# One-hot gate rows made token by token, and expert numbers found pair by pair, in a one-core PEER block

## The chip, the cores and the metric

The kernel runs on one core of a Trainium2 chip. The metric is device time in microseconds, as the median of several runs; lower is better. The engines are called by their names here: TensorE (PE in the profile, PEld for its weight loads), VectorE (DVE), ScalarE (ACT), GpSimd (POOL) and SyncE (SP), which issues most of the DMAs.

## The reference, cut to what matters

One layer of a bidirectional encoder: 512 tokens of width 1024 go through a mixer (a gated recurrence and a long convolution), and then through PEER, a channel mixer that looks up single-neuron experts. The change lies in PEER. For each token and each of 8 heads it finds the best 16 of 128 sub-keys in each of two halves, adds them to 256 candidate pairs, keeps the best 16 pairs, and so has 128 experts a token out of 16384, each with a softmax gate:

```python
s1, i1 = lax.top_k(s[:, :, 0], PEER_TOPK)
s2, i2 = lax.top_k(s[:, :, 1], PEER_TOPK)
cand_s = s1[..., :, None] + s2[..., None, :]          # 16 x 16 pairs
cand_i = i1[..., :, None] * PEER_NKEYS + i2[..., None, :]
top_s, pos = lax.top_k(cand_s, PEER_TOPK)
experts = jnp.take_along_axis(cand_i, pos, axis=-1)
g = jax.nn.softmax(top_s, axis=-1)
act = jax.nn.gelu(jnp.einsum('td,thkd->thk', xb, u[experts])) * g
out = jnp.einsum('thk,thkd->td', act, v[experts])
```

## The kernel before, in words

Four blocks of 128 tokens go through the layer. Block 0 (`GTB`) fetches its experts' rows by indirect DMA. Blocks 1 to 3 (`DTB`, 384 tokens) go the dense way: the products with all 16384 experts are made row by row (128 rows of 128 experts, `act_row`), a dense matrix of gates that is zero but for the chosen experts is multiplied in, and the rows of `v` are summed by matmuls into three accumulators (`combine`). All large matmuls are made of three passes with operands split in a high and a low part (`mm3`, `split`); the low parts are VectorE's work, except those of `uT` in the last loop, which are GpSimd's.

`top16` finds the best 16 of a row and their places by five VectorE operations. Only 50 of the 256 pairs can be among the best 16 (`PAIRS`), and a choice of rank under 8 only among the first 20 of them (`NFIRST`).

`select(tb, part)` serves half of the heads (4) of one token block, so it is called eight times. It adds up scores (`cs`) and expert numbers (`ci`) of the 50 pairs, takes the best 16 (`ctop`, `cpos`), makes the softmax `gate`, and then reads the expert number at each place. Before the change it does so for two heads and eight choices at a time: `one` compares the pair identities `pio` with the places (L1188), `exp` multiplies by `ci` (L1190), and a reduction over the pairs gives `eid` (L1181); the reductions run up to `ahead` groups later. A piece of it ends at each `yield`; the number that is yielded is a planner's cost.

`gates_out(k, tb)` turns the 128 experts and gates of each token into the token's 128 x 128 gate matrix. The expert number is parted in a row number `i1` and a column number `i2` (L1207 to L1211), both and the gates are transposed so that tokens lie along the free dimension (`tr` in bf16 for the numbers, `tg` for the gates), and then four tokens at a time are made: `one` compares the iota with both numbers (L1228), ScalarE turns the first half into `rows` (L1230), and VectorE multiplies the second half by the gates into `own` (L1231). Four blocks (`LAG`) later TensorE multiplies `own` and `rows` for each token (L1238), ScalarE copies the result to `Gs` (L1243), and SyncE's queue writes it to DRAM (`Gd`).

The order is set by generators. `queries` makes the sub-key scores and runs the first-half selections of blocks 1 and 2 beside them. Then `weave(main(), fill, PER)` (L894) runs the second-half selection of block 1 and `gates_out` for the three blocks, with the remaining selections put in after every third block of four tokens (`mixed`, L892), and lets one `act_row` in for each 2.4 units of the costs that are yielded. The last loop, `weave(rows(), gathered(), 1.0)` (L1023), runs all `combine` and the remaining `act_row` with the work of block 0 in between: its top-16 and its two selections (L917), then the indirect gathers (L906), one `scalar_tensor_tensor` with a written-out sum for each of 128 gathered rows of `u` (L931) and one for each of `v` (L940). An engine's queue runs in its order.

Of the kernel before, what the change touches and what calls it, by code (L numbers as in the profile page):

```python
# [9 lines left out]
F32 = mybir.dt.float32  # L10
# [11 lines left out]
P = 128  # L22
# [6 lines left out]
TOPK = 16  # L29
# [780 lines left out]
def peer(C, ctx, mh, ml):  # L810
# [6 lines left out]
    eid = cp.tile([P, TB, P], F32, name="eid")  # L817
    v16 = cp.tile([P, TB, 16, TOPK], F32, name="v16")
    i16 = cp.tile([P, TB, 16, TOPK], U32, name="i16")
    pio = cp.tile([P, NPAIR, TOPK // 2], BF16, name="pio")  # L820
    with tc.tile_pool(name="pid", bufs=1) as ip:
        pid = ip.tile([P, NPAIR], F32, name="pid")
        nc.scalar.dma_start(pid, a["pair"].to_broadcast([P, NPAIR]))
        nc.vector.tensor_copy(pio, pid[:, :, None].to_broadcast([P, NPAIR, TOPK // 2]))
    iota = cp.tile([P, P, 4], BF16, name="iota")
    nc.gpsimd.iota(iota, pattern=[[1, P], [0, 4]], base=0, channel_multiplier=0, allow_small_or_imprecise_dtypes=True)  # L826
    gidx = cp.tile([P, P], I32, name="gidx")
    gdot = cp.tile([P, P], F32, name="gdot")
    gw = cp.tile([P, P], F32, name="gw")
    def chosen(pool, tb, part, ahead=2):  # L830
        return select(C, pool, tb, part, v16, i16, gate, eid, pio, ahead)

    projected(C, mh, ml, xh, xl, xg)
    rowctx = ExitStack()
# [50 lines left out]
    with tc.tile_pool(name="slw", bufs=2) as sw, tc.tile_pool(name="gb", bufs=1) as gb, \  # L885
            tc.tile_pool(name="go", bufs=3) as go, tc.tile_pool(name="ps_g", bufs=5, space=PSUM) as ps_g:
        def main():
            rest = [[chosen(sw, tb, part) for part in range(2) if part or k >= EARLY] for k, tb in enumerate(DTB)]
            yield from chain(*rest[0])
            for k, tb in enumerate(DTB):  # L890
                nxt = chain(*rest[k + 1]) if k + 1 < len(DTB) else iter(())
                yield from mixed(gates_out(C, gb, go, ps_g, k, tb, gate, eid, iota), nxt, MIX)  # L892

        weave(main(), fill, PER)  # L894

# [14 lines left out]
    def gathered():  # L910

        for part in range(2):
            for hp in range(part * HEADS, part * HEADS + HEADS):
                top16(C, sw, v16[:, GTB, hp], i16[:, GTB, hp], s0[:, hp])
                if hp % 2:
                    yield 3.2
            yield from chosen(sw, GTB, part, 1)  # L917
        sgctx.close()
        nc.vector.tensor_copy(gidx, eid[:, GTB])
        swctx.close()  # L920
        gp = rowctx.enter_context(tc.tile_pool(name="gp", bufs=GBUFS))
        asked = chain(((a["u"], j) for j in range(P)), ((a["v"], j) for j in range(P)))
        there = [gather(gp, *q) for q in islice(asked, GAHEAD)]

        def row():
            there.extend(gather(gp, *q) for q in islice(asked, 1))
            return there.pop(0)

        for j in range(P):
            t = row()  # L930
            nc.vector.scalar_tensor_tensor(t, t, 1.0, xg, op0=ALU.mult, op1=ALU.mult, accum_out=gdot[:, j : j + 1])  # L931
            yield 1.2
        nc.scalar.activation(gw, gdot, AF.Gelu_apprx_tanh)
        nc.vector.tensor_mul(gw, gw, gate[:, GTB])
        for j in range(P):
            t = row()
            if j == 0:
                nc.vector.tensor_scalar(gacc, t, gw[:, 0:1], None, op0=ALU.mult)
            else:
                nc.vector.scalar_tensor_tensor(gacc, t, gw[:, j : j + 1], gacc, op0=ALU.mult, op1=ALU.add)  # L940
            yield 1.2
# [192 lines left out]
           for x in range(a0, a0 + na) for y in range(b0, b0 + nb)]  # L1134


def select(C, w2, tb, part, v16, i16, gate, eid, pio, ahead=2):

    nc = C.nc
    H = HEADS // 2  # L1140
    hs = slice(part * 2 * H, part * 2 * H + 2 * H)
    ks = slice(part * H * TOPK, part * H * TOPK + H * TOPK)
    i16f = w2.tile([P, 2 * H, TOPK], F32, name="i16f")
    nc.vector.tensor_copy(i16f, i16[:, tb, hs])
    ctop = w2.tile([P, H, TOPK], F32, name="ctop")
    cpos = w2.tile([P, H, TOPK], U32, name="cpos")
    cs = w2.tile([P, H, NPAIR], F32, name="cs")
    ci = w2.tile([P, H, NPAIR], F32, name="ci")
    i1x = w2.tile([P, H, TOPK], F32, name="i1x")
    vv = v16[:, tb, hs].rearrange("p (h q) k -> p h q k", q=2)  # L1150
    ii = i16f.rearrange("p (h q) k -> p h q k", q=2)
    nc.vector.tensor_scalar(i1x, ii[:, :, 0], 128.0, None, op0=ALU.mult)
    for dst, x1, x2, groups in ((cs, vv[:, :, 0], vv[:, :, 1], pair_groups(0, TOPK)[0]), (ci, i1x, ii[:, :, 1], FIRST + OTHERS)):
        for a0, na, b0, nb, off in groups:
            nc.vector.tensor_tensor(  # L1155
                dst[:, :, off : off + na * nb].rearrange("p h (a b) -> p h a b", b=nb),
                x1[:, :, a0 : a0 + na, None].to_broadcast([P, H, na, nb]),
                x2[:, :, None, b0 : b0 + nb].to_broadcast([P, H, na, nb]), op=ALU.add)
    yield 2.0
    for hd in range(H):  # L1160
        top16(C, w2, ctop[:, hd], cpos[:, hd], cs[:, hd])
    yield 2.5

    ex = w2.tile([P, H, TOPK], F32, name="ex")
    sm = w2.tile([P, H], F32, name="sm")
    mx = w2.tile([P, H], F32, name="mx")
    nc.vector.tensor_reduce(mx, ctop, axis=AX.X, op=ALU.max)
    nc.vector.tensor_tensor(ex, ctop, mx[:, :, None].to_broadcast([P, H, TOPK]), op=ALU.subtract)
    nc.scalar.activation(ex, ex, AF.Exp)
    nc.vector.reduce_sum(sm, ex, axis=AX.X)  # L1170
    nc.vector.reciprocal(sm, sm)
    nc.vector.tensor_tensor(gate[:, tb, ks].rearrange("p (h k) -> p h k", k=TOPK), ex,
                            sm[:, :, None].to_broadcast([P, H, TOPK]), op=ALU.mult)
    cpf = w2.tile([P, H, TOPK], BF16, name="cpf")
    nc.vector.tensor_copy(cpf, cpos)
    yield 1.0
    found = []

    def reduce():
        out, ex = found.pop(0)  # L1180
        nc.vector.reduce_sum(out, ex, axis=AX.X)  # L1181

    H2, K2 = 2, TOPK // 2
    for hd in range(0, H, H2):
        for k0, n in ((0, NFIRST), (K2, NPAIR)):
            one = w2.tile([P, H2, NPAIR, K2], BF16, name="one", bufs=2)
            ex = w2.tile([P, H2, K2, NPAIR], F32, name="exp", bufs=ahead + 1)
            nc.vector.tensor_tensor(one[:, :, :n], pio[:, None, :n].to_broadcast([P, H2, n, K2]),  # L1188
                                    cpf[:, hd : hd + H2, None, k0 : k0 + K2].to_broadcast([P, H2, n, K2]), op=ALU.is_equal)
            nc.vector.tensor_mul(ex[:, :, :, :n], one[:, :, :n].rearrange("p h j k -> p h k j"),  # L1190
                                 ci[:, hd : hd + H2, None, :n].to_broadcast([P, H2, K2, n]))
            out = eid[:, tb, ks].rearrange("p (h k) -> p h k", k=TOPK)[:, hd : hd + H2, k0 : k0 + K2]
            found.append((out, ex[:, :, :, :n]))
            if len(found) > ahead:
                reduce()
            yield 0.7 if k0 == 0 else 1.3
    while found:
        reduce()


def gates_out(C, gb, go, ps_g, k, tb, gate, eid, iota):

    nc = C.nc
    i1 = gb.tile([P, P], F32, name="i1")
# [5 lines left out]
    nc.vector.tensor_sub(i1, eid[:, tb], i2)  # L1210
    nc.vector.tensor_scalar(i1, i1, 1.0 / 128, None, op0=ALU.mult)  # L1211

    tr = gb.tile([P, P // 4, 2, 4], BF16, name="tr", bufs=2)
    tg = gb.tile([P, P], F32, name="tg", bufs=2)
    pt = ps_g.tile([P, 512], F32, name="ps_g")
    for j, src in enumerate((i1, i2, gate[:, tb])):
        nc.tensor.transpose(pt[:, j * P : j * P + P], src, C.ident)
    nc.scalar.copy(tr.rearrange("p b j t -> p j b t"), pt[:, : 2 * P].rearrange("p (j b t) -> p j b t", j=2, t=4))
    nc.scalar.copy(tg, pt[:, 2 * P : 3 * P])
    NB = P // 4  # L1220
    made, prods = {}, {}
    for b in range(NB + LAG + 1):
        if b < NB:

            one = go.tile([P, 2, P, 4], BF16, name="one", bufs=3)
            rows = go.tile([P, 4, P], F32, name="rows", bufs=LAG + 2)
            own = go.tile([P, 4, P], F32, name="own", bufs=LAG + 2)
            nc.vector.tensor_tensor(one, iota[:, None].to_broadcast([P, 2, P, 4]),  # L1228
                                    tr[:, b, :, None, :].to_broadcast([P, 2, P, 4]), op=ALU.is_equal)
            nc.scalar.copy(rows, one[:, 0].rearrange("p i t -> p t i"))  # L1230
            nc.vector.tensor_tensor(own, one[:, 1].rearrange("p i t -> p t i"),  # L1231
                                    tg[:, b * 4 : b * 4 + 4, None].to_broadcast([P, 4, P]), op=ALU.mult)
            made[b] = rows, own
        if LAG <= b < NB + LAG:
            rows, own = made.pop(b - LAG)
# [133 lines left out]
```

## Time and profile before

| | |
|---|---|
| time, median of 3 runs | 2113.68 us (2111.99 to 2114.71) |
| the profiled execution's own time | 2113.9 us |
| its span, first to last instruction | 2112.1 us |
| TensorE busy | 2058.7 us (97%) |
| VectorE busy | 1736.1 us (82%) |
| ScalarE busy | 978.6 us (46%) |
| GpSimd busy | 638.2 us (30%) |
| mean granted TensorE clock | 0.992 of full speed |

All stretches are in microseconds from the span's first instruction. A busy time is the union of the printed durations of an engine's instructions in a stretch; matmuls are pipelined, so that a busy TensorE is not TensorE at its peak. In a row of instructions "out<-in" are the kernel's names for the tiles, and "128x512 f32" is partitions by elements.

### The profile page before, as it was taken

The page shows a single profiled execution, that of the slowest core. Times are in us where ns is not written, and L with a number is a line of the kernel's source. Part 1 is how long each engine was busy: PE and PEld are TensorE (multiplying, and loading weights), DVE is VectorE, ACT ScalarE, POOL GpSimd, SP SyncE. Part 2 cuts the span into 40 slices and gives each one's busy share as a digit, 9 for nine tenths or more (in the row PEclk, how much of TensorE's full clock was granted, in tenths as well). Part 3 has the DMA queues.
Part 4 walks back from the last instruction along what each step waited for, and adds up shares of the span by engine and source line. Part 5 has one row for each costly group of instructions (what it writes and reads, how often), then busy time and mean ns, then how long its engine had stood idle before and what let it go on. Part 6 is the DMA issues. An engine that isn't in the chain of part 4 may idle for free. (4 is left out here: it accounts for less than half of the span.)

```text
span 2112.1 us, 29790 instructions
## 1 busy us (share of the span) xinstructions
PE 2058.7 (97%) x11109; PEld 1822.7 (86%) x11109; DVE 1736.1 (82%) x3073; ACT 978.6 (46%) x1396; POOL 638.2 (30%) x361
## 2 busy tenths in 40 slices
PE   7999999999999999979999999999999999999998
PEld 6888888888888898879988989989989998998997
DVE  6888764998998546999999988878878879778785
ACT  6555434667665623337766423333333333333333
POOL 0000000000000000000000378877777676666760
PEclk9999999999999999999999999999999999999999
DMA  6212222222212444124547689988888988888884
GB/s 199 80 51 66 70 70 94 67 65 66 70 54 81 120 151 139 61 70 168 202 180 250 192 311 344 327 318 304 321 318 301 317 311 299 316 317 324 296 286 148
DMA packets 153949, 407.68 MB, mean 193 GB/s; under 512 B 12457, under 2 KB 65451, under 8 KB 152140
## 3 DMA queue, kind: packets, MB, share of 16 engines
q1 hardware_dynamic: 110028, 255.98, 35.8%
q0 software_dynamic: 36864, 134.23, 17.6%
q10 hardware_dynamic: 6912, 15.56, 2.1%
q8 instruction: 87, 1.43, 0.3%
q14 instruction: 58, 0.48, 0.1%
HBM read 373.22 MB, written 32.51 MB: 192 GB/s over the span
## 5 line engine op out<-in xcount | busy, mean ns | idle before, releaser
L86 POOL TENSOR_TENSOR ul<-uraw,uh 128x1024 fp32r<-128x1024 f32 x100 | 265.3, 2654 | 589.7 <-DMA uraw<-in_uT 387.6
L95 PE MATMUL ps_a<-pxl,uh 128*128 128x384 f32 x1008 | 343.1, 340 | 0.0
L94 PE MATMUL ps_a<-pxh,uh 128*128 128x384 f32 x1008 | 341.8, 339 | 1.3 <-ACT gact L867 1.2
L980 PE MATMUL acc<-vl,gh 128*128 128x512 f32 x768 | 301.5, 393 | 2.1 <-DVE vl L86 2.1
L979 PE MATMUL acc<-vh,gh 128*128 128x512 f32 x768 | 299.7, 390 | 2.6 <-ACT vh L85 2.6
L981 PE MATMUL acc<-vh,gl 128*128 128x512 f32 x768 | 301.5, 393 | 0.0
L94 PE MATMUL ps_mm<-xh,whi 128*128 128x512 f32 (+1 forms) x656 | 259.1, 396 | 1.5 <-ACT xh L195 1.2
L940 DVE SCALAR_TENSOR_TENSOR xg<-grow,gw,xg 128x1024 f32<-128x1024 f32 x127 | 208.6, 1643 | 63.1 <-DMA grow<-in_v,gidx 62.0
L931 DVE SCALAR_TENSOR_TENSOR grow<-grow,xg 128x1024 f32<-128x1024 f32 x128 | 195.9, 1541 | 73.6 <-DMA grow<-in_u,gidx 73.3
L95 PE MATMUL ps_mm<-xl,whi 128*128 128x512 f32 (+1 forms) x656 | 255.0, 390 | 0.3 <-DVE xl L196 0.3
L85 ACT CAST vh<-vraw 128x1024 fp32r<-128x1024 f32 x128 | 134.3, 1050 | 252.7 <-PE acc L981 179.7
L826 POOL IOTA iota<- 128x512 bf16 x1 | 1.2, 1237 | 754.4 <-DVE gt L281 754.4
L906 POOL DMA_INDIRECT grow<-in_u,gidx x128 | 201.0, 1570 | 41.4 <-issue 19.4
L97 PE MATMUL ps_a<-pxh,ul 128*128 128x384 f32 x1008 | 200.1, 338 | 6.3 <-DVE ul L86 4.1
L85 ACT CAST uh<-uraw 128x1024 fp32r<-128x1024 f32 x128 | 134.7, 1053 | 143.5 <-PE ps_a L95 76.5
L94 PEld LDWEIGHTS ps_a<-pxh,uh 128*128 128x128 f32 x1008 | 191.1, 190 | 6.4 <-ACT gact L867 2.2
L95 PEld LDWEIGHTS ps_a<-pxl,uh 128*128 128x128 f32 x1008 | 190.9, 189 | 3.8
L86 DVE TENSOR_TENSOR vl<-vraw,vh 128x1024 fp32r<-128x1024 f32 x128 | 186.4, 1457 | 8.3 <-ACT vh L85 8.3
L97 PEld LDWEIGHTS ps_a<-pxh,ul 128*128 128x128 f32 x1008 | 176.8, 189 | 8.2 <-DVE ul L86 5.5
L906 POOL DMA_INDIRECT grow<-in_v,gidx x128 | 170.5, 1332 | 32.7 <-issue 18.3
L85 ACT CAST whi<-wraw 128x1024 fp32r<-128x1024 f32 x112 | 117.3, 1050 | 131.0 <-PE ps_mm L95 123.5
L980 PEld LDWEIGHTS acc<-vl,gh 128*128 128x128 f32 x768 | 144.6, 188 | 31.1 <-DVE vl L86 2.9
(414 smaller groups left out, 4188.8 us busy)
## 6 DMA issues: line engine op xcount, KB each, us to landing
uraw<-in_uT SPq DMA_DIRECT2D x128, 512.0 KB, 7.0
vraw<-in_v SPq DMA_DIRECT2D x128, 512.0 KB, 6.3
wraw<-in_w_in SPq DMA_DIRECT2D x80, 512.0 KB, 3.6
Gd<-Gs SPq DMA_DIRECT2D x12, 2048.0 KB, 7.2
gt<-Gd SPq DMA_DIRECT2D x32, 768.0 KB, 8.7
wraw<-in_w_q SPq DMA_DIRECT2D x16, 512.0 KB, 4.0
wraw<-in_w_b SPq DMA_DIRECT2D x8, 512.0 KB, 3.6
wraw<-in_w_a SPq DMA_DIRECT2D x8, 512.0 KB, 4.3
```

Of the source, the lines that this page charges most:

```text
L85: nc.scalar.copy(hi, src)
L86: return (eng or nc.vector).tensor_sub(lo, src, hi).ins
L94: nc.tensor.matmul(out, ah, bh, start=(i == 0), stop=False)
L95: nc.tensor.matmul(out, *((al, bh) if late else (ah, bl)), start=False, stop=False)
L97: nc.tensor.matmul(out, *((ah, bl) if late else (al, bh)), start=False, stop=(stop and i == n - 1))
L826: nc.gpsimd.iota(iota, pattern=[[1, P], [0, 4]], base=0, channel_multiplier=0, allow_small_or_imprecise_dtypes=True)
L906: nc.gpsimd.indirect_dma_start(out=t, out_offset=None, in_=tab, in_offset=bass.IndirectOffsetOnAxis(ap=gidx[:, j : j + 1], axis=0))
L931: nc.vector.scalar_tensor_tensor(t, t, 1.0, xg, op0=ALU.mult, op1=ALU.mult, accum_out=gdot[:, j : j + 1])
L940: nc.vector.scalar_tensor_tensor(gacc, t, gw[:, j : j + 1], gacc, op0=ALU.mult, op1=ALU.add)
L979: nc.tensor.matmul(acc[k][:, c], gh[:, ts_], vh[:, ds_], start=(r == 0), stop=False)
L980: nc.tensor.matmul(acc[k][:, c], gh[:, ts_], vl[:, ds_], start=False, stop=False)
L981: nc.tensor.matmul(acc[k][:, c], gl[:, ts_], vh[:, ds_], start=False, stop=(r == NK - 1))
```

## The change

In `gates_out` the one-hot for the column number is no longer compared four tokens at a time and then multiplied: one `tensor_scalar` per token compares a row of numbers 0 to 127 (`line`) with the token's column number and multiplies by its gate, both read from memory as one value per partition. `one` shrinks to the half that `rows` needs. In `select` the three steps over groups become one `scalar_tensor_tensor` for each head and choice: compare the pair identities with the place, multiply by the expert numbers, and write out the sum.

```diff
@@ -817,18 +817,17 @@
     eid = cp.tile([P, TB, P], F32, name="eid")
     v16 = cp.tile([P, TB, 16, TOPK], F32, name="v16")
     i16 = cp.tile([P, TB, 16, TOPK], U32, name="i16")
-    pio = cp.tile([P, NPAIR, TOPK // 2], BF16, name="pio")
-    with tc.tile_pool(name="pid", bufs=1) as ip:
-        pid = ip.tile([P, NPAIR], F32, name="pid")
-        nc.scalar.dma_start(pid, a["pair"].to_broadcast([P, NPAIR]))
-        nc.vector.tensor_copy(pio, pid[:, :, None].to_broadcast([P, NPAIR, TOPK // 2]))
+    pio = cp.tile([P, NPAIR], F32, name="pio")
+    nc.scalar.dma_start(pio, a["pair"].to_broadcast([P, NPAIR]))
     iota = cp.tile([P, P, 4], BF16, name="iota")
     nc.gpsimd.iota(iota, pattern=[[1, P], [0, 4]], base=0, channel_multiplier=0, allow_small_or_imprecise_dtypes=True)
+    line = cp.tile([P, P], F32, name="line")
+    nc.gpsimd.iota(line, pattern=[[1, P]], base=0, channel_multiplier=0, allow_small_or_imprecise_dtypes=True)
     gidx = cp.tile([P, P], I32, name="gidx")
     gdot = cp.tile([P, P], F32, name="gdot")
     gw = cp.tile([P, P], F32, name="gw")
-    def chosen(pool, tb, part, ahead=2):
-        return select(C, pool, tb, part, v16, i16, gate, eid, pio, ahead)
+    def chosen(pool, tb, part):
+        return select(C, pool, tb, part, v16, i16, gate, eid, pio)
 
     projected(C, mh, ml, xh, xl, xg)
     rowctx = ExitStack()
@@ -889,7 +888,7 @@
             yield from chain(*rest[0])
             for k, tb in enumerate(DTB):
                 nxt = chain(*rest[k + 1]) if k + 1 < len(DTB) else iter(())
-                yield from mixed(gates_out(C, gb, go, ps_g, k, tb, gate, eid, iota), nxt, MIX)
+                yield from mixed(gates_out(C, gb, go, ps_g, k, tb, gate, eid, iota, line), nxt, MIX)
 
         weave(main(), fill, PER)
 
@@ -914,7 +913,7 @@
                 top16(C, sw, v16[:, GTB, hp], i16[:, GTB, hp], s0[:, hp])
                 if hp % 2:
                     yield 3.2
-            yield from chosen(sw, GTB, part, 1)
+            yield from chosen(sw, GTB, part)
         sgctx.close()
         nc.vector.tensor_copy(gidx, eid[:, GTB])
         swctx.close()
@@ -1134,7 +1133,7 @@
            for x in range(a0, a0 + na) for y in range(b0, b0 + nb)]
 
 
-def select(C, w2, tb, part, v16, i16, gate, eid, pio, ahead=2):
+def select(C, w2, tb, part, v16, i16, gate, eid, pio):
 
     nc = C.nc
     H = HEADS // 2
@@ -1171,34 +1170,21 @@
     nc.vector.reciprocal(sm, sm)
     nc.vector.tensor_tensor(gate[:, tb, ks].rearrange("p (h k) -> p h k", k=TOPK), ex,
                             sm[:, :, None].to_broadcast([P, H, TOPK]), op=ALU.mult)
-    cpf = w2.tile([P, H, TOPK], BF16, name="cpf")
+    cpf = w2.tile([P, H, TOPK], F32, name="cpf")
     nc.vector.tensor_copy(cpf, cpos)
     yield 1.0
-    found = []
-
-    def reduce():
-        out, ex = found.pop(0)
-        nc.vector.reduce_sum(out, ex, axis=AX.X)
-
-    H2, K2 = 2, TOPK // 2
-    for hd in range(0, H, H2):
-        for k0, n in ((0, NFIRST), (K2, NPAIR)):
-            one = w2.tile([P, H2, NPAIR, K2], BF16, name="one", bufs=2)
-            ex = w2.tile([P, H2, K2, NPAIR], F32, name="exp", bufs=ahead + 1)
-            nc.vector.tensor_tensor(one[:, :, :n], pio[:, None, :n].to_broadcast([P, H2, n, K2]),
-                                    cpf[:, hd : hd + H2, None, k0 : k0 + K2].to_broadcast([P, H2, n, K2]), op=ALU.is_equal)
-            nc.vector.tensor_mul(ex[:, :, :, :n], one[:, :, :n].rearrange("p h j k -> p h k j"),
-                                 ci[:, hd : hd + H2, None, :n].to_broadcast([P, H2, K2, n]))
-            out = eid[:, tb, ks].rearrange("p (h k) -> p h k", k=TOPK)[:, hd : hd + H2, k0 : k0 + K2]
-            found.append((out, ex[:, :, :, :n]))
-            if len(found) > ahead:
-                reduce()
-            yield 0.7 if k0 == 0 else 1.3
-    while found:
-        reduce()
-
-
-def gates_out(C, gb, go, ps_g, k, tb, gate, eid, iota):
+
+    out = eid[:, tb, ks].rearrange("p (h k) -> p h k", k=TOPK)
+    for hd in range(H):
+        for k in range(TOPK):
+            n = NFIRST if k < TOPK // 2 else NPAIR
+            own = w2.tile([P, NPAIR], F32, name="own", bufs=4)
+            nc.vector.scalar_tensor_tensor(own[:, :n], pio[:, :n], cpf[:, hd, k : k + 1], ci[:, hd, :n],
+                                           op0=ALU.is_equal, op1=ALU.mult, accum_out=out[:, hd, k : k + 1])
+        yield 0.9
+
+
+def gates_out(C, gb, go, ps_g, k, tb, gate, eid, iota, line):
 
     nc = C.nc
     i1 = gb.tile([P, P], F32, name="i1")
@@ -1210,26 +1196,26 @@
     nc.vector.tensor_sub(i1, eid[:, tb], i2)
     nc.vector.tensor_scalar(i1, i1, 1.0 / 128, None, op0=ALU.mult)
 
-    tr = gb.tile([P, P // 4, 2, 4], BF16, name="tr", bufs=2)
-    tg = gb.tile([P, P], F32, name="tg", bufs=2)
+    tr = gb.tile([P, P // 4, 4], BF16, name="tr", bufs=2)
+    tg = gb.tile([P, 2, P], F32, name="tg", bufs=2)
     pt = ps_g.tile([P, 512], F32, name="ps_g")
     for j, src in enumerate((i1, i2, gate[:, tb])):
         nc.tensor.transpose(pt[:, j * P : j * P + P], src, C.ident)
-    nc.scalar.copy(tr.rearrange("p b j t -> p j b t"), pt[:, : 2 * P].rearrange("p (j b t) -> p j b t", j=2, t=4))
-    nc.scalar.copy(tg, pt[:, 2 * P : 3 * P])
+    nc.scalar.copy(tr, pt[:, :P].rearrange("p (b t) -> p b t", t=4))
+    nc.scalar.copy(tg, pt[:, P : 3 * P].rearrange("p (j t) -> p j t", j=2))
     NB = P // 4
     made, prods = {}, {}
     for b in range(NB + LAG + 1):
         if b < NB:
 
-            one = go.tile([P, 2, P, 4], BF16, name="one", bufs=3)
+            one = go.tile([P, P, 4], BF16, name="one", bufs=3)
             rows = go.tile([P, 4, P], F32, name="rows", bufs=LAG + 2)
             own = go.tile([P, 4, P], F32, name="own", bufs=LAG + 2)
-            nc.vector.tensor_tensor(one, iota[:, None].to_broadcast([P, 2, P, 4]),
-                                    tr[:, b, :, None, :].to_broadcast([P, 2, P, 4]), op=ALU.is_equal)
-            nc.scalar.copy(rows, one[:, 0].rearrange("p i t -> p t i"))
-            nc.vector.tensor_tensor(own, one[:, 1].rearrange("p i t -> p t i"),
-                                    tg[:, b * 4 : b * 4 + 4, None].to_broadcast([P, 4, P]), op=ALU.mult)
+            nc.vector.tensor_tensor(one, iota, tr[:, b, None, :].to_broadcast([P, P, 4]), op=ALU.is_equal)
+            nc.scalar.copy(rows, one.rearrange("p i t -> p t i"))
+            for q in range(4):
+                t = b * 4 + q
+                nc.vector.tensor_scalar(own[:, q], line, tg[:, 0, t : t + 1], tg[:, 1, t : t + 1], op0=ALU.is_equal, op1=ALU.mult)
             made[b] = rows, own
         if LAG <= b < NB + LAG:
             rows, own = made.pop(b - LAG)
```

## Rows read from the trace of the kernel before

**Rows 1.** The busy line of the page: busy us (share of the span) xinstructions.
```profile
PE 2058.7 (97%) x11109; PEld 1822.7 (86%) x11109; DVE 1736.1 (82%) x3073; ACT 978.6 (46%) x1396; POOL 638.2 (30%) x361
```

**Rows 2.** Busy time by stage: us, PE, PEld, DVE, ACT, POOL, PEclk, DMA share, GB/s.
```profile
870.00:948.00 78.00, 68.87 (x352) 60.24 (x350) 78.00 (x368) 26.86 (x44) 0.00 (x0) 0.98 0.19 63
948.00:1136.00 188.00, 178.77 (x1237) 170.38 (x1238) 186.39 (x463) 144.19 (x245) 0.00 (x0) 0.96 0.51 189
1136.00:1160.00 24.00, 20.57 (x117) 19.93 (x115) 23.49 (x113) 9.29 (x12) 4.86 (x2) 0.99 0.85 296
1300.00:2000.00 700.00, 700.00 (x3496) 631.62 (x3496) 571.88 (x500) 250.31 (x294) 505.24 (x287) 1.00 0.88 315
```

**Rows 3.** The chain that ended last, in order of time: start us, us, what.
```profile
1133.71 0.53 DVE i L1254 x2
...
1159.66 1.12 DVE vl L86
1160.83 0.80 PE acc L980
...
1221.59 8.25 DMA grow<-in_u,gidx
```

**Rows 4.** VectorE in order of time, blocks of `gates_out`: start us, us printed, instruction.
```profile
953.18 1.29 DVE L1231 TENSOR_TENSOR own<-one,tg 128x512 f32<-128x512 bf16 x2
954.39 1.28 DVE L1228 TENSOR_TENSOR one<-iota,tr 128x1024 bf16<-128x1024 bf16 x2
955.59 1.28 DVE L1231 TENSOR_TENSOR own<-one,tg 128x512 f32<-128x512 bf16 x2
```

**Rows 5.** VectorE groups by form, whole span: count, busy us, mean ns, idle before.
```profile
L1231 DVE TENSOR_TENSOR own<-one,tg 128x512 f32<-128x512 bf16 x96 | 62.6, 682 | 0.0
L1228 DVE TENSOR_TENSOR one<-iota,tr 128x1024 bf16<-128x1024 bf16 x96 | 62.4, 682 | 0.4 <-ACT rows L1230 0.4
```

**Rows 6.** VectorE in order of time, ahead of the first gate block.
```profile
949.21 0.21 DVE L1211 TENSOR_SCALAR i<-i 128x128 f32<-128x128 f32 x1
949.34 1.04 DVE L1155 TENSOR_TENSOR ci<-i1x,i16f 128x32 f32<-128x32 f32 x11
```

**Rows 7.** VectorE groups by form, relatives of the new instructions, whole span.
```profile
L748 DVE SCALAR_TENSOR_TENSOR ya<-hrs,vec,so 128x512 f32<-128x512 f32 x8 | 5.9, 741 | 0.0
L747 DVE TENSOR_TENSOR hrs<-ps_x,hrs 128x512 f32<-128x512 f32 x8 | 5.5, 683 | 1.0 <-ACT hrs L116 1.0
...
L1155 DVE TENSOR_TENSOR ci<-i1x,i16f 128x8 f32<-128x8 f32 x16 | 1.9, 164 | 0.0
...
L375 DVE TENSOR_SCALAR arg<-ps_x,vec 64x512 f32<-64x512 f32 x2 | 1.6, 800 | 3.5 <-PE ps_x L389 3.5
```

**Rows 8.** VectorE groups by form in 870 to 948 us, the selection's.
```profile
L1190 DVE TENSOR_TENSOR exp<-one,ci 128x800 f32<-128x800 bf16 x6 | 9.6, 1596 | 0.0
...
L1181 DVE TENSOR_REDUCE eid<-exp 128x16 f32<-128x800 f32 x6 | 5.9, 978 | 0.0
L1190 DVE TENSOR_TENSOR exp<-one,ci 128x320 f32<-128x320 bf16 x6 | 4.3, 718 | 0.0
L1188 DVE TENSOR_TENSOR one<-pio,cpf 128x800 bf16<-128x800 bf16 x6 | 3.4, 568 | 0.0
L1181 DVE TENSOR_REDUCE eid<-exp 128x16 f32<-128x320 f32 x6 | 2.8, 471 | 0.0
...
L1188 DVE TENSOR_TENSOR one<-pio,cpf 128x320 bf16<-128x320 bf16 x6 | 1.9, 315 | 0.0
```

**Rows 9.** VectorE in order of time, an instruction with a sum in the last loop.
```profile
1238.00 1.21 DVE L86 TENSOR_TENSOR vl<-vraw,vh 128x1024 fp32r<-128x1024 f32 x1
1239.13 1.21 DVE L931 SCALAR_TENSOR_TENSOR grow<-grow,xg 128x1024 f32<-128x1024 f32 x1
1240.28 0.08 DVE L931 DVE_READ_ACCUMULATOR grow<-grow,xg 128x1 f32 x1
1240.28 1.22 DVE L931 SCALAR_TENSOR_TENSOR grow<-grow,xg 128x1024 f32<-128x1024 f32 x1
```

## The prediction

> **What bounds the kernel now.** I read the busy line of the page first. TensorE is busy 97% of the span, VectorE 82% [rows 1]. A mean over the span hides the stage that matters, so the second view was the busy time by stages, cut where the lines of the diff begin and end. From 870 to 948 us (two of the early selections and the third) VectorE is busy 78.00 of 78 us and TensorE 68.87. From 948 to 1136 us (the gate matrices) VectorE has 186.39 of 188 and TensorE 178.77. From 1136 to 1160 us it is 23.49 of 24 against 20.57, and in the steady part behind it TensorE has no gap while VectorE has room [rows 2]. So the reader sees one engine full for 290 us, and that is VectorE, with TensorE close behind. The third view was the chain of waits: from 1133.71 us it runs from one VectorE instruction to the next, until `vl` at 1159.66 releases the first product of the last loop; at 1221.59 it runs through the first gathered row, and that gather cannot start until the expert numbers of token block 0 are known [rows 3]. Everything the diff touches on VectorE lies between 870 and 1221 us. I take it that a microsecond added there is a microsecond at the end, while a microsecond removed is worth at most what TensorE idles.
>
> **The unit of the sum.** A printed duration is longer than the place that an instruction takes. Two `own` in a row are printed as 1.29 us, yet the next pair starts 1.21 us behind them [rows 4]. So neighbours overlap by 0.08 us, and I count start to start. Two `one` and two `own` take 955.59 - 953.18 = 2.41 us, 1.205 us for a block of four tokens [rows 4]; there are 96 of each [rows 5].
>
> **Gate matrices, `gates_out`.** Removed per block: one `one` over 1024 and one `own` over 512 elements, 1.205 us. Added: `one` over 512 elements, and four `tensor_scalar` over 128 elements with two scalars read from memory each. The 1024 bf16 elements take no longer than 512 f32 ones, two a cycle, and the new `one` has the same inner pattern; 256 cycles fewer at 0.96 a ns are 0.267 us off 0.60, which leaves 0.333. The plain 128-element f32 `tensor_scalar` with constants starts at 949.21 and its follower at 949.34: 0.13 us [rows 6]. What the scalars from memory add is read from longer relatives: 512 elements with one such scalar take 741 ns against 683 without (58 more), and the one `tensor_scalar` with two takes 800, 117 above the 683 of a one-a-cycle instruction [rows 7]. So an `own` of one token takes 0.13 + 0.12 = 0.25 us, four take 1.00, and the block 1.333 us: 0.128 more than before. Times 96: **+12.3 us**. Bounds: below, the scalars cost nothing in a short instruction (0.853 a block, -33.8 us); above, the comparison with two scalars runs at one element a cycle, 64 cycles or 0.067 us more four times (+25.6 on top, +37.9). I take the middle because the row with two scalars is the nearest, and it shows them paid in full.
>
> **Expert numbers, `select`.** Eight calls, two for each token block. Removed per call: two rounds of six instructions, printed 315, 718, 471, 568, 1596 and 978 ns [rows 8], 4.65 us, less six overlaps of 0.08, so 4.17 a round and 8.33 a call. Added per call: 64 `scalar_tensor_tensor` (4 heads by 16 choices), 32 over 20 pairs and 32 over 50, each with one scalar from memory and a sum written out. The smallest two-input instruction has 8 elements and takes 164 ns [rows 7], so 156 ns are there before the first element. With 1.04 ns an element and 58 for the scalar, less 80 of overlap, 20 pairs take 0.155 us and 50 take 0.186: 32 x 0.341 = 10.9 us. The sum is a second instruction, the accumulator read. Behind the 1024-element relative it is printed with 0.08 us, but the next instruction starts at the same moment, and start to start is 1.15 against 1.13 for the `vl` without a sum [rows 9], so I count 0.008 each, 0.5 us a call. That makes 11.4 a call, 3.1 more than before; eight calls, **+24.7 us**. Bounds: below, a free scalar (7.2 us, -1.1 a call, -9); above, the accumulator read takes its own 0.08 behind a short instruction, where no long stream covers it (+4.4 a call, +35 on top).
>
> The Vector Engine (DVE) Microarchitecture Reference of the Trainium skill ("Points that are easy to get wrong") says that a scalar-tensor-tensor with two SBUF sources that are not bf16 runs at half throughput, since no read port is left for the accumulator; the new instruction is of that kind. The row of 1024 elements has two such sources and a sum, and its 1.15 us are one element a cycle, so the trace disagrees. By that rule the eight calls would cost 8 x 2240 elements x 1.04 ns = 18.6 us more.
>
> **Edits that I cost at nothing.** The cast of `pio` (0.4 us) goes from VectorE, well ahead of the full stretch; I leave it out. The second iota is GpSimd's, which is idle until the last loop [rows 2]. The copies on ScalarE swap widths (`tr` half, `tg` double) and keep their count. Half of the `one` being gone, `rows` may start 0.27 us earlier; nothing comes of it, because VectorE fills that time. No wait is added: the products still run four blocks behind `own`. The weights that the selection yields fall from 4.0 to 3.6, which moves the total that paces the fill rows from 55.9 to 55.3; divided by 2.4, both give 23 rows. The same DMAs are issued in the same order.
>
> **Sum.** 12.3 + 24.7 = 37 us on VectorE. Three selections (9.3) fall into 870 to 948 us and three (9.3) with the gates (12.3) into 948 to 1136, both full. The last two (6.2) stand ahead of the first gather, and `vl` of the following rows is queued behind the instruction that waits for that gather. So nothing hides them: where TensorE now idles 9 us in each of the first two stages it will idle longer. The profiled execution took 2113.9 us (span 2112.1), 0.2 above the median of the three runs. 2113.9 + 37 = 2151; the removed cast and the few tenths in which VectorE does wait today make it **2150 us**.
>
> **Rivals.**
> A. The accumulation is dearer than the long row shows: the read takes its 0.08 us each time (2150 + 35 = 2185), or, as the page's rule would have it, the stream runs at half speed (2150 + 19 = 2169). For it: the read is an instruction of its own with a printed time, and a 20-element stream is shorter than that. Against it: behind 1024 elements it leaves no trace. An `own` at one element a cycle (+26, 2176) has the same sign and size.
> B. The second scalar is free: `own` takes 0.19 us, the block 1.093, and the gates gain 10.8 us instead of losing 12.3. Then 2150 - 23 = 2127. For it: two scalars could be fetched together. Against it: 117 ns is twice 58.
> C. Faster: the scalars of a short instruction are fetched under its predecessor, as its start-up partly is. Then the block takes 0.853 us and a call 7.2, and VectorE loses 43 us of work. The gain is cut off by TensorE: 9.2 us idle in 948 to 1136, 3.4 from three selections before, 2.3 from the two behind; 15 us, 2099. It decides where a 128-element `own` gets below 0.22 us and a pair instruction below 0.13. Against it: both rows with scalars show them paid although a full instruction ran ahead of them.
> D. VectorE's longer queue is hidden: TensorE, not VectorE, holds the stage from 948 to 1136, since the two are 8 us apart, and the selections are caught up later in the loop, where VectorE has 18% free. Then only what exceeds TensorE's gaps counts and about 2115 comes out. Against it: the chain at 1133 to 1160 is VectorE alone, and the first product waits for it.
>
> **How the numbers follow.** The forecast has 0.58 (2134 to 2163 its own range), A 0.18, B 0.11, C 0.07, D 0.06. The range 2122 to 2188 takes in A and B and leaves out C and D and a heap of A's prices. Within 0.2% is 2109.5 to 2117.9, about what a measurement of this kernel can tell from no change. Faster gets 0.07 (C), the same 0.06 (D), slower 0.87.
>
> **What would show it.** In the profile of the changed kernel: `own` of one token at 0.32 us printed and 0.25 start to start; pair instructions at 0.155 and 0.186 start to start, and the accumulator read printed without moving its follower; 870 to 948 longer by about 9 us, the gate stage by about 21, with TensorE's idle time there up by as much; the loop behind the first gather as long as now. If start to start of `own` is under 0.22, or the first `vl` stands no later than 1159.66, the argument is wrong.

## The result and the profile after

The changed kernel takes 2141.06 us (median of 4 runs, 2139.92 to 2141.78), the kernel before 2114.19 on the same chip: 1.0128 times as long, interval 1.0111 to 1.0146, or 27 us. The forecast was 2150, 37 us more. The profiled execution took 2141.01 us, span 2139.2.

The busy line, which answers to [rows 1]; VectorE has 20.6 us more, TensorE the same share:
```profile
PE 2065.9 (97%) x11109; PEld 1824.2 (85%) x11109; DVE 1756.7 (82%) x4288; ACT 982.4 (46%) x1396; POOL 634.3 (30%) x362
```
The busy time by stages (columns as in [rows 2]), cut where the same work begins and ends:
```profile
870.00:966.00 96.00, 85.11 (x413) 74.13 (x412) 93.25 (x774) 28.88 (x49) 0.00 (x0) 0.93 0.16 52
966.00:1177.00 211.00, 184.59 (x1226) 169.11 (x1226) 209.48 (x1099) 148.36 (x246) 0.00 (x0) 0.98 0.45 169
1177.00:1201.00 24.00, 21.07 (x122) 20.68 (x120) 23.89 (x156) 9.91 (x13) 7.21 (x3) 1.00 0.69 257
1300.00:2000.00 700.00, 699.82 (x3517) 633.46 (x3516) 572.51 (x520) 253.28 (x298) 510.83 (x290) 1.00 0.90 319
```
VectorE is still the full engine there, and TensorE's idle time in the gate stage has grown from 9.2 us [rows 2] to 26.4. Ahead of the gate stage it has hardly grown, from 9.1 to 10.9. The new instructions as groups by form (count, busy us, mean ns printed), the answer to [rows 5, 8]:
```profile
L1218 DVE TENSOR_SCALAR own<-line,tg 128x128 f32<-128x128 f32 x384 | 109.5, 366 | 0.0
L1182 DVE SCALAR_TENSOR_TENSOR own<-pio,cpf,ci 128x50 f32<-128x50 f32 x256 | 54.6, 289 | 0.0
L1182 DVE SCALAR_TENSOR_TENSOR own<-pio,cpf,ci 128x20 f32<-128x20 f32 x256 | 53.6, 279 | 0.0
L1182 DVE DVE_READ_ACCUMULATOR own<-pio,cpf,ci 128x1 f32 x512 | 49.0, 96 | 0.0
L1214 DVE TENSOR_TENSOR one<-iota,tr 128x512 bf16<-128x512 bf16 x96 | 42.4, 442 | 0.0
```
Read by printed means, one block would take 0.442 + 4 x 0.366 = 1.9 us. The order in time tells another price (start us, us printed):
```profile
1005.40 0.25 DVE L1182 SCALAR_TENSOR_TENSOR own<-pio,cpf,ci 128x20 f32<-128x20 f32 x1
1005.55 0.10 DVE L1182 DVE_READ_ACCUMULATOR own<-pio,cpf,ci 128x1 f32 x1
1005.55 0.25 DVE L1182 SCALAR_TENSOR_TENSOR own<-pio,cpf,ci 128x20 f32<-128x20 f32 x1
...
1006.87 0.29 DVE L1182 SCALAR_TENSOR_TENSOR own<-pio,cpf,ci 128x50 f32<-128x50 f32 x1
1007.06 0.10 DVE L1182 DVE_READ_ACCUMULATOR own<-pio,cpf,ci 128x1 f32 x1
1007.06 0.29 DVE L1182 SCALAR_TENSOR_TENSOR own<-pio,cpf,ci 128x50 f32<-128x50 f32 x1
...
1008.21 0.44 DVE L1214 TENSOR_TENSOR one<-iota,tr 128x512 bf16<-128x512 bf16 x1
1008.55 1.13 DVE L1218 TENSOR_SCALAR own<-line,tg 128x128 f32<-128x128 f32 x4
1009.57 0.44 DVE L1214 TENSOR_TENSOR one<-iota,tr 128x512 bf16<-128x512 bf16 x1
```
From one `one` to the next is 1009.57 - 1008.21 = 1.36 us (1.205 before [rows 4]); four `own` take 1.02 of it, 0.256 each. A pair instruction takes 0.160 us for 20 pairs and 0.192 for 50, and its accumulator read starts together with the next pair instruction: it takes no place at all. A call comes to 32 x 0.352 = 11.26 us.

Where the 27 us arise is read from four marks, in tile views (least, median and longest ns; first and last start). Before:
```profile
L1228 DVE TENSOR_TENSOR one<-iota,tr x96: 670/680/704, 952.0 to 1130.7; 128x1024 bf16<-128x1024 bf16 x96
L919 DVE CAST gidx<-eid x1: 213/213/213, 1221.1 to 1221.1; 128x128 int32<-128x128 f32 x1
L979 PE MATMUL acc<-vh,gh x768: 387/389/632, 1158.7 to 2103.8; 128*128 128x512 f32 x192
```
And after:
```profile
L1214 DVE TENSOR_TENSOR one<-iota,tr x96: 405/438/476, 968.2 to 1171.7; 128x512 bf16<-128x512 bf16 x96
L918 DVE CAST gidx<-eid x1: 223/223/223, 1254.5 to 1254.5; 128x128 int32<-128x128 f32 x1
L978 PE MATMUL acc<-vh,gh x768: 389/389/628, 1200.7 to 2130.9; 128*128 128x512 f32 x192
```
The first gate block is 16.2 us late, the last 41.0, the first product of the last loop 42.0, the gather's indices (`gidx`) 33.4, the last product 27.1. So VectorE's price arrives in full, and more, at the last loop; 9 us come back before the gather and 6 behind it.

Of the first 16.2 us, 6 are there before any of the changed VectorE instructions runs; 1.4 of these 6 stand already in the mixer, where the two kernels do the same work (its `yb` starts at 296.1 us against 294.7 before). ScalarE's queue in the kernel before (`ACTq` rows are DMA issues):
```profile
703.07 0.33 ACTq L823 DMA_DIRECT2D pid<-in_pair  x1
...
753.30 0.33 ACTq L1069 DMA_DIRECT2D h<-in_x  x1
```
The same queue after:
```profile
756.03 0.33 ACTq L821 DMA_DIRECT2D pio<-in_pair  x1
756.40 0.46 ACTq L1063 DMA_DIRECT2D gfn<-in_g_ffn  x1
756.47 0.61 ACT L85 CAST mgh<-gt 128x512 fp32r<-128x512 f32 x1
756.88 1.04 ACTq L1068 DMA_DIRECT2D h<-in_x  x2
```
And what waits for `h` (idle time before an instruction, and its releaser, in brackets): VectorE before, VectorE after, then TensorE after:
```profile
758.64 0.88 DVE L1074 TENSOR_TENSOR h<-ps_mm,h 128x256 f32<-128x256 f32 x2
```
```profile
765.92 1.09 DVE L1073 TENSOR_TENSOR h<-ps_mm,h 128x256 f32<-128x256 f32 x3 [7.06 <-DMA h<-in_x]
```
```profile
766.40 0.58 PE L94 MATMUL ps_mm<-woh,mgh 128*128 128x256 f32 x1 [3.01 <-DVE h L1073]
```
`pio` is now loaded straight into a tile of the long-lived pool, and its DMA goes out at 756.03 instead of 703.07. I read this as a wait for memory that the stage before still holds; the trace names no releaser, but e1 and e7 show that the tile's pool decides it. `h`, whose first load was issued at 753.30, now stands behind it in ScalarE's queue and is issued 3.6 us later.

### The profile page after: what moved, and what is told of

It is laid out like the page before. It is cut to its first block, busy times and chain, and to the rows that moved or that the text cites. A ratio compares the mean times of both kernels' runs of the same rounds, so it can differ in the third digit from the quotient of the medians.

```text
span 2139.2 us, 30909 instructions
## 1 busy us (share of the span) xinstructions
PE 2065.9 (97%) x11109; PEld 1824.2 (85%) x11109; DVE 1756.7 (82%) x4288; ACT 982.4 (46%) x1396; POOL 634.3 (30%) x362
## 4 chain that ended last, share of the span: by engine, by line
PE 72%; DVE 19%; ACT 4%; issue 2%; DMA 2%; POOL 1%; ACTq 0%; DVEq 0%; POOLq 0%
PE acc L979 8%; PE acc L980 7%; PE acc L978 7%; PE ps_mm L97 7%; PE ps_mm L95 7%; PE ps_mm L94 7%; PE ps_a L97 6%; PE ps_a L94 6%; PE ps_a L95 6%; DVE own L1182 4%; DVE own L1218 3%; PE ps_x L718 2%; PE ps_g L1224 1%; PE ps_x L94 1%; PE ps_x L97 1%
## 5 line engine op out<-in xcount | busy, mean ns | idle before, releaser
L930 DVE SCALAR_TENSOR_TENSOR grow<-grow,xg 128x1024 f32<-128x1024 f32 x128 | 201.4, 1585 | 68.2 <-DMA grow<-in_u,gidx 67.8
L939 DVE SCALAR_TENSOR_TENSOR xg<-grow,gw,xg 128x1024 f32<-128x1024 f32 x127 | 203.1, 1599 | 65.2 <-DMA grow<-in_v,gidx 64.1
L905 POOL DMA_INDIRECT grow<-in_u,gidx x128 | 196.7, 1537 | 44.3 <-issue 22.5
L980 PEld LDWEIGHTS acc<-vh,gl 128*128 128x128 f32 x768 | 144.6, 188 | 30.2
```

What stands on the lines that cost most here:

```text
L905: nc.gpsimd.indirect_dma_start(out=t, out_offset=None, in_=tab, in_offset=bass.IndirectOffsetOnAxis(ap=gidx[:, j : j + 1], axis=0))
L980: nc.tensor.matmul(acc[k][:, c], gl[:, ts_], vh[:, ds_], start=False, stop=(r == NK - 1))
```

## The experiments

**e1, the queue's order put back.** A staging tile as before, the rest as changed:
```diff
-    nc.scalar.dma_start(pio, a["pair"].to_broadcast([P, NPAIR]))
+    with tc.tile_pool(name="pid", bufs=1) as ip:
+        pid = ip.tile([P, NPAIR], F32, name="pid")
+        nc.scalar.dma_start(pid, a["pair"].to_broadcast([P, NPAIR]))
+        nc.vector.tensor_copy(pio, pid)
```


> The changed kernel, with the pair identities loaded into a staging tile of their own pool and copied to pio by VectorE, as the kernel before did. Theory Q (ScalarE's queue): the load straight into pio waits for memory that the mixer still holds, and the loads of h queue behind it; with the staging the loads of h go out as early as before, the stretch of the output projection is 6 us shorter again, and the time is 2135 us (2133 to 2137). Rival (the 6 us belong to another order that the longer program was given, not to this load): no change, 2141 us.

The load goes out at 704.08 us again. Measured 2136.89 us (2135.08 to 2139.14), 1.0108 [1.0091, 1.0124] against before: 4.2 less than the changed kernel and within theory Q's range. With four runs a side that spread over 2 and 4 us, the 4.2 are good to some 2 us. The place of this load is worth about 4 us of the 27; the other 23 belong to the new instructions.

**e2, the new `gates_out` alone**, in the kernel before:

> The kernel before, with the new gates_out alone. Theory V (VectorE is full between 870 and 1221 us and hands on what is added): a block takes 1.36 instead of 1.205 us, 96 blocks 14.8 us more until the first product of the last loop; up to a third is given back in the loop; 2124 to 2129 us. Rival T (TensorE holds this stage, and 9 us of its idle time take the addition in): 2114 to 2119 us.

2126.89 us (2123.26 to 2127.54), 1.0064 [1.0047, 1.0081]: +13.1, with +14.8 by start to start (96 x 0.154), within theory V's range. The price is passed on almost whole.

**e3, the new `select` alone**, staged as in e1:

> The kernel before, with the new select alone (pair identities staged as before). Theory V: a call takes 11.3 instead of 8.3 us, eight calls 23.5 us more, of which the loop gives back up to a third; 2129 to 2137 us, and with the gates alone it adds up to the changed kernel with staged identities. Rival T: the selections are caught up later, 2114 to 2122 us.

2123.91 us (2123.11 to 2126.18), 1.0051 [1.0035, 1.0068]: +10.1, between the two ranges, so neither expectation held. Priced start to start it is +23.5, so 13 us came back; together with e2's it makes e1's 23. The trace names the way back. VectorE from 820 to 870 us, before and then e3 (columns as in [rows 2]):
```profile
820.00:870.00 50.00, 49.90 (x248) 41.04 (x247) 44.59 (x273) 17.30 (x32) 0.00 (x0) 1.00 0.27 87
```
```profile
820.00:870.00 50.00, 49.91 (x247) 40.91 (x246) 49.62 (x307) 17.01 (x31) 0.00 (x0) 1.00 0.32 94
```
Ahead of the full stretch VectorE used to idle 5.4 us. With the new `select` the last three of the five operations of `top16` stand there seven times more (5.7 us start to start), ahead of the first selection in VectorE's order; they fill the idle time and are then missing between the last gate block and `gidx`. Four more us come from the gating of one row that is now behind `gidx`, where VectorE has room, and 3 from the last loop. That makes 12 of the 13. The 128 pair instructions that run beside GpSimd in the last two selections take 35 us start to start, where as many beside an idle GpSimd take 22; the old instructions lose some 6 us there too, and others (`cs`, `gate`, `vl`) now lose less. Why the order came out so was not tried.

**e4, `own` with constants in place of the scalars from memory** (on e1; the gate matrices then hold no gates):
```diff
-    nc.vector.tensor_scalar(own[:, q], line, tg[:, 0, t : t + 1], tg[:, 1, t : t + 1], op0=ALU.is_equal, op1=ALU.mult)
+    nc.vector.tensor_scalar(own[:, q], line, float(t), 0.0625, op0=ALU.is_equal, op1=ALU.mult)
```


> The changed kernel with staged identities, and the tensor_scalar of own compares with a constant and multiplies by a constant instead of the two values from memory (so the gate matrices hold no real gates). Theory P (the scalars from memory cost 0.06 us each): own falls from 0.256 to 0.135 us start to start, VectorE loses 46 us in the gate stage, and the time falls by what TensorE idles there, to 2105 to 2116 us. Rival I (a short instruction takes 0.25 us whatever its scalars): no change against the staged kernel, 2135 us.

2101.47 us, 0.9942 [0.9925, 0.9958]: 35.4 below e1, under every expectation. In the trace:
```profile
1006.19 0.63 DVE L1221 TENSOR_SCALAR own<-line 128x128 f32<-128x128 f32 x4
1006.74 0.42 DVE L1217 TENSOR_TENSOR one<-iota,tr 128x512 bf16<-128x512 bf16 x1
```
Four take 0.55 us, 0.135 each (median start to start), against 0.256: the two scalars cost 0.121 us, 46 us over the kernel. Three quarters of that reach the end, which comes 12 us earlier than in the kernel before; rival C of the prediction put the bound at 15.

**e5, the pair instruction with a constant place** (on e1; the expert numbers are then those of fixed places):
```diff
-            nc.vector.scalar_tensor_tensor(own[:, :n], pio[:, :n], cpf[:, hd, k : k + 1], ci[:, hd, :n],
+            nc.vector.scalar_tensor_tensor(own[:, :n], pio[:, :n], float(k), ci[:, hd, :n],
```


> The changed kernel with staged identities, and the pair instruction compares with a constant instead of the place from memory (so the expert numbers are those of fixed pairs). Theory P: it falls from 0.160 and 0.192 to 0.10 and 0.134 us start to start, 512 of them lose 30 us, and the time is 2107 to 2117 us, no slower than the kernel before. Rival A (the written-out sum is what makes it dear): start to start stays above 0.15, and the time at 2133 to 2136 us.

2107.45 us, 0.997 [0.9959, 0.9981]: 29.4 below e1, for 512 x 0.060 = 31 us off VectorE (0.100 and 0.131 us start to start, against 0.160 and 0.192). The gathers then fetch other rows, but 25.7 us are there at the first product of the last loop, ahead of any gather (1168.1 against 1193.8 in e1). The scalar is the cost; the accumulation stays in, and its read still takes no place.

**e6, a fifth `own` in each block** (one of four made twice, on e1):
```diff
-            for q in range(4):
+            for q in (0, 1, 2, 3, 0):
```


> The changed kernel with staged identities, and in each block the own of the first token is made a second time (same result): 96 more instructions of 0.256 us, 24.6 us of VectorE time in the gate stage and nothing else. Theory V: the first product of the last loop comes 24 us later and the end 16 to 25 us, 2151 to 2160 us. Rival T (the stage is as long as TensorE's work): under 8 us, 2135 to 2143 us.

2160.88 us (2160.59 to 2161.48), 1.0223 [1.0208, 1.0239]: +24.0 over e1 for 96 x 0.256 = 24.6 us. In the gate stage VectorE's time is passed on one to one; that TensorE holds the stage is out.

**e7, the late `h` alone.** The kernel before, its staging tile taken from the long-lived pool:
```diff
-    with tc.tile_pool(name="pid", bufs=1) as ip:
-        pid = ip.tile([P, NPAIR], F32, name="pid")
+    pid = cp.tile([P, NPAIR], F32, name="pid")
```


> The kernel before, with its staging tile taken from the pool of the PEER part instead of a pool of its own; all else as it was. Theory Q: its load now waits for the memory that the mixer holds, the loads of h queue behind it on ScalarE, and the output projection is 5 to 6 us longer: 2119 to 2120 us. Rival: no change, 2114 us.

2113.21 us (2108.12 to 2115.77), 0.9998 [0.9989, 1.0007]: no change, so the expected 6 us were wrong. Yet the load went out at 754.74, and `h` was late:
```profile
763.92 1.08 DVE L1073 TENSOR_TENSOR h<-ps_mm,h 128x256 f32<-128x256 f32 x3 [5.24 <-DMA h<-in_x]
```
But less late than in the changed kernel: the first transpose of `h` starts at 791.3 us, against 788.6 before and 794.5 after, and the first product of the last loop is 1.0 us late. So this run repeats less than half of the delay and does not price it; the price is e1's 4.2 us. Why the same wait is shorter here stays open, and so does whether VectorE's idle time from 820 to 870 us, which the changed kernel has spent (48.65 busy of 50), would have taken the whole delay up.

**e8 and e9, can VectorE be relieved in the gate stage?** Both are the kernel before. In e8 GpSimd, idle in that stage, makes `own` in every second block:
```diff
-            nc.vector.tensor_tensor(own, one[:, 1].rearrange("p i t -> p t i"),
+            (nc.gpsimd if b % 2 else nc.vector).tensor_tensor(own, one[:, 1].rearrange("p i t -> p t i"),
```


> The kernel before, with one edit: in every second block of four tokens the multiplication that makes `own` is GpSimd's instead of VectorE's. Nothing is left out. Theory V (VectorE's time between 948 and 1136 us is time at the end, down to what TensorE needs): VectorE loses 48 x 0.60 = 29 us, GpSimd, idle in that stage, gets 48 instructions of about 1.3 us each (half of the 2.65 us that its 1024-element subtraction takes in the last loop). The gain is cut off by TensorE's 9.2 us idle in the stage and a few us behind it, as in the run with constant scalars, which ended 12 us under the kernel before: 2102 us (2098 to 2107). Rival C (GpSimd and VectorE disturb each other): VectorE's small instructions take about three times as long in the stretch from 1131 us on, where GpSimd works, as before it; 63 us of GpSimd's work at half of VectorE's pace would cost 30 us and take the gain back: 2112 us or more, with `one` printed well over 0.68 us beside GpSimd's `own`.

2118.64 us (2116.63 to 2121.37), 1.0026 [1.0017, 1.0035]: 0.26% slower, although VectorE was rid of 48 instructions, as rival C expected. First the groups between 948 and 1136 us, then the order in time, GpSimd's rows and VectorE's in a fence each:
```profile
L1228 DVE TENSOR_TENSOR one<-iota,tr 128x1024 bf16<-128x1024 bf16 x93 | 82.5, 922 | 2.1 <-POOL own L1231 1.9
L1231 POOL TENSOR_TENSOR own<-one,tg 128x512 f32<-128x512 bf16 x46 | 73.5, 1600 | 304.0 <-ACT rows L1230 230.4 <-DVE one L1228 65.4 <-PE ps_a L95 3.1
```
```profile
1004.00 1.34 POOL L1231 TENSOR_TENSOR own<-one,tg 128x512 f32<-128x512 bf16 x1 [1.32 <-DVE one L1228]
```
```profile
1003.76 0.68 DVE L1231 TENSOR_TENSOR own<-one,tg 128x512 f32<-128x512 bf16 x1
1004.36 1.54 DVE L1228 TENSOR_TENSOR one<-iota,tr 128x1024 bf16<-128x1024 bf16 x1
```
GpSimd's `own` ends at 1005.34. VectorE's `one`, started at 1004.36, ends at 1005.90: 0.56 us of it come after GpSimd's end, about what it takes alone (0.68 printed, 0.60 start to start), so until then it got little or nothing done. In the mean `one` is printed with 922 ns instead of 682 [rows 5]. The Trainium skill says in "SBUF — State Buffer", "SBUF: two separate sides", that the port pair which the two engines share is an exclusive lock, which the one that starts first holds for its whole instruction. The rows agree.

In e9 ScalarE makes `own` in every fourth block:
```diff
+            if b % 4 == 3:
+                for q in range(4):
+                    nc.scalar.activation(own[:, q], one[:, 1, :, q], AF.Copy, scale=tg[:, b * 4 + q : b * 4 + q + 1])
+            else:
```


> The kernel before, with one edit: in every fourth block of four tokens `own` is made by ScalarE, token by token, as a copy scaled by one value per partition (24 blocks, 96 instructions of 128 elements). Nothing is left out. Theory V: VectorE loses 24 x 0.60 = 14.4 us in a stage in which TensorE idles 9.2 us; ScalarE goes from 144 to about 170 busy us of 188: 2104 us (2101 to 2108). Rival S (ScalarE is the next one late: its `rows` and its copies `Gs` stand behind the new instructions, and TensorE's products wait for them): no gain, 2110 to 2118 us, with TensorE's waits put down to ScalarE instead of VectorE.

2108.0 us (2106.74 to 2109.03), 0.9974 [0.9964, 0.9984]: 5 us below the kernel before, at the edge of theory V's range, and the only complete version here that beats both kernels. The stage, as in [rows 2]:
```profile
948.00:1136.00 188.00, 174.95 (x1240) 169.74 (x1241) 177.59 (x459) 166.76 (x341) 0.00 (x0) 0.99 0.52 194
```
VectorE now has 10 us of room; ScalarE has 21 and TensorE idles 13. TensorE's waits are spread over both engines, so rival S holds in part. The last gate block is 7 us earlier, but one more `act_row` stands ahead of the first product, which is 6 us later; the loop has that row less to do.

## Why the prediction was right, and where it was not

The direction and its cause were right: VectorE is full where the change adds to it (e6: 24.0 of 24.6 us arrive). The prices held. `own` was put at 0.25 us and takes 0.256, the block at 1.333 and takes 1.36; the pair instructions at 0.163 and 0.194 with the accumulator read, and take 0.160 and 0.192. The sum on VectorE is 14.8 + 23.5 = 38 us where 37 were forecast. That each scalar from memory is paid in full in a short instruction was read from two longer relatives [rows 7]; e4 and e5 show it: 0.121 us for two, 0.060 for one. Rivals A and B fall by the same rows: the accumulator read takes no place, 30 pairs more cost 0.032 us, which is one element a cycle and no half speed, and the second scalar is paid. C's condition (scalars hidden under the predecessor) is refuted by e4. D's first half, that TensorE holds the gate stage, falls by e6; its second half, that selections are caught up, holds for 13 of 23.5 us (e3).

Three steps failed, and the time is inside the range all the same.

"The same DMAs are issued in the same order." They are not: the tile that went was a staging tile in a pool of its own, and without it the load goes out 53 us later and holds `h` up behind it on ScalarE's queue. Cost 4.2 us (e1), which the prediction had at nothing.

"So nothing hides them", of the six selections before the gates' end and the last two. It held for the gates (13.1 of 14.8 in e2), not for the selections (10.1 of 23.5 in e3). The prediction looked at VectorE's time from 870 us on, where it is full, and not at 820 to 870, where it idles 5.4 us and could take work ahead. From the last gate to `gidx` it expected 6 us more and got 7.6 less. Nor is that stretch on the path that it named: `gidx` comes 33.4 us later than before, but from the first product to the last TensorE is busy 929.4 of 930.6 us, and what it waits for are the first `vh` and `vl`, nothing that stands behind the gather.

"The loop behind the first gather as long as now." It is 6.3 us shorter (884.7 against 891.0 to the span's end). One more `act_row` stands ahead of the first product in TensorE's queue. That order is made when the kernel is built; e9, where VectorE has less to do, has the extra row too, so it is no effect of VectorE's lateness on the chip. Matmuls on `ps_a` from 870 us to the first product, before and after:
```profile
870.00:1158.60 288.60, 135.42 (x672) 0.97 0.46 165
```
```profile
870.00:1200.60 330.60, 151.53 (x696) 0.96 0.39 142
```
(The columns are the stretch, its length, TensorE's busy time on these, the granted clock, DMA share and GB/s.) 24 matmuls are one row, 24 x 0.174 = 4.2 us that the loop no longer has to do. The start of the loop stalls less too. The 140 us behind the first product, before and after (columns as in [rows 2]):
```profile
1160.00:1180.00 20.00, 19.17 (x85) 17.28 (x86) 20.00 (x15) 10.79 (x14) 12.80 (x4) 0.85 0.66 206
1180.00:1230.00 50.00, 48.35 (x244) 43.61 (x242) 41.76 (x117) 18.61 (x23) 15.13 (x9) 1.00 0.64 197
1230.00:1300.00 70.00, 68.98 (x334) 61.83 (x335) 64.27 (x70) 22.14 (x27) 59.90 (x33) 0.98 0.93 336
```
```profile
1201.00:1221.00 20.00, 19.12 (x88) 16.85 (x88) 20.00 (x70) 12.49 (x16) 9.05 (x4) 0.91 0.79 273
1221.00:1271.00 50.00, 49.89 (x250) 44.72 (x249) 45.84 (x218) 16.14 (x19) 20.87 (x13) 1.00 0.70 230
1271.00:1341.00 70.00, 69.82 (x352) 63.00 (x351) 61.92 (x69) 25.02 (x32) 58.41 (x32) 1.00 0.95 343
```
TensorE idles 3.5 us there before and 1.2 after, and its mean granted clock in the first 20 us is 0.91 of full speed instead of 0.85. Counted on TensorE, from the first product to the last, the loop is 14.9 us shorter (930.2 against 945.1): the row and the idle time make about half of it, and the rest was not taken apart.

The account of the traces, by the four marks: 6.0 ahead of the changed instructions, 10.2 to the first gate block (9.3 forecast), 24.8 in the gate stage (21.6), -7.6 to `gidx` (+6.2), -6.3 behind it (0): 27.1 us. The misses have both signs, and it is partly luck that they leave a time only 9 us under the forecast. One sign that the prediction named did not come: TensorE's idle time ahead of the gate stage grew by 1.8 us and not by 9; it ran 413 matmuls there instead of 352, at a granted clock of 0.93 instead of 0.98.

## What to carry to other kernels

Price a short VectorE instruction start to start, and add 0.06 us for each scalar that it reads from memory: here many short instructions with scalars lost to a few long ones, though they do fewer elements, and without the scalars they would have won (e4, e5). Where an engine is full over a stretch, look also at the stretch before: what idles there can take work ahead. Before a staging tile is taken away, ask when the memory of the new target comes free, and what is queued behind the load.

## What the runs showed of the hardware

The accumulator read of a `scalar_tensor_tensor` starts with the next instruction, also behind streams of 20 elements; its printed 0.096 us is no place in the queue. A scalar from memory costs 0.06 us in an instruction of 20 elements as in one of 512 (e5, [rows 7]). A bf16 comparison of 1024 elements all but stands still while GpSimd's multiplication runs (1.54 us in place of 0.68 in e8), so that work given to the idle GpSimd made the kernel slower.
